# Tile-by-tile ends, quartered projection weights, spread POOL splits in a one-layer hybrid encoder step

## The chip, the core and the metric

The kernel runs on one core of a Trainium2 chip. A core has a matrix engine (TensorE, PE in the profile, with its weight loads as PEld) and three elementwise engines: VectorE (DVE), ScalarE (ACT) and GpSimd (POOL). The sync engine (SP) issues the DMA transfers. Each engine works through its own queue in order, and semaphores tie the queues together. The metric is the device time of one execution in microseconds (us). Smaller is better.

## The reference

One layer on 1024 prompt frames and 64 frames of a running stream, model width 1024, all in float32:

```python
hp = macaron_half(xp, ln1_g, ln1_b, ffn1_w_gate, ffn1_w_up, ffn1_w_down)
qa, ka, va, qi, ki, wi, qb, kb, vb, lfb = project(hp, pos, w_in, b_f)
mp = mixer(qa, ka, va, qi, ki, wi, qb, kb, vb, lfb)
hp = layer_norm(ALPHA * hp + mp @ w_out, ln2_g, ln2_b)
xp = macaron_half(hp, ln3_g, ln3_b, ffn2_w_gate, ffn2_w_up, ffn2_w_down)
...
def macaron_half(x, g, b, w_gate, w_up, w_down):
    return layer_norm(ALPHA * x + 0.5 * swiglu(x, w_gate, w_up, w_down), g, b)
```

The feed-forward width is 2816. The mixer has eight heads A (sparse: an indexer scores all keys with a weighted sum of Relus and the best 256 are attended, with a partial rotary embedding on the first 16 of 64 dimensions) and eight heads B (forgetting attention with a cumulative log gate). The new keys, values and gates are outputs too.

## The kernel before

**Tiles.** The 1088 rows are nine tiles t = 0..8 of 128 rows; tile 8 holds the 64 streaming rows. Each float32 factor of a product is split into a high part (a cast on ACT into the matmul type) and a low part (value minus high, on DVE or POOL; `split`, line 107), and a product is three matmuls: high x high, low x high, high x low. In the names an h or l at the end marks the parts: wh and wl, mh and ml.

**Feed-forward.** Each of the two feed-forward blocks is `ffn_a` (gate and up, line 203) and `ffn_b` (down, line 591). Both use a Strassen-like scheme over blocks of tiles 0 to 3 and 4 to 7: operand sums such as T1, T2, T3, T4 are made once, in `Strassen.put` (line 167), by subtracting a tile's normed row block zz and its partner's, fetched again from DRAM as zt. `body0` (line 258) is the first piece of `ffn_a`; its matmuls are called fa0 (fa in the profile), fs for the sample tile, fy for what follows, and its intermediate copies p are taken from PSUM by ACT into the buffers "ssum" (four of them). `ffn_b` runs seven products P1, P2, P3, P6, P5, P7, P4, each over six pairs of blocks of the inner dimension and four tiles; the matmuls are called fbP, with weights mh, ml and hidden values lh, ll. The first pairs of a product go over all four tiles in turn, its last `late` ones tile by tile, so that a tile's result is added (`evict`, line 674) while the next tile runs. With the last product, P4, the rows get their final norm (`finish`, `ln_tail`: lines 529 to 541 on DVE) and go out as y_prompt.

**Projection.** `in_proj` (line 1047) goes through eleven groups of columns of w_in, at most 328 wide, each over the tiles. `load_w` (973) fetches and splits the weights of the next group when tile `ahead` has been issued: as two blocks (wst) or three (ist), whose cast and subtraction stand in the queues at that place. Beside groups 2 and 3 run the indexer's scores, `idx_step`: matmuls iq, the Relu `rt` on ACT (line 1144), and sums on DVE and POOL. `rope_apply` (945) rotates a tile's heads with six small operations. `tsplit` (1061) transposes results through PSUM (ts...), from where ACT takes them (hl, ft).

**Attention and w_out.** Attention works through units of heads and query blocks, jobs B first and then jobs A. POOL scales each unit's exponentials e by 1/sum (line 1681). Outputs of jobs B are parked in DRAM and fetched again while jobs A run (`fetch_out`, name kept); POOL splits them into xh and xl (lines 1697 and 1698). After that `gemm_b` (432) multiplies with w_out in three groups of three tiles, adds the residual and norms (`zz_post`), and `emit_s` (1991 ff.) writes each tile to h2d and puts it into the operands of the second feed-forward.

**Order.** The order on each engine is drawn up when the program is built, by the framework's scheduler from the program order and its own cost estimates. The code sets priorities by where a step is written: generators put on `todo` are advanced by `pump` between matmuls, and `tc.issue_after(x)` holds an instruction behind x. A tile of a buffer pool waits until the buffer's last user is done.

Of the kernel before, what the change touches and what calls it, by code (L numbers as in the profile page):

```python
# [47 lines left out]
def hybrid_step(ctx: ExitStack, tc: tile.TileContext, i, o):  # L48
# [57 lines left out]

    def split(hi, lo, src):
        S.copy(hi, src)  # L108
        V.tensor_tensor(lo, src, f(hi), ALU.subtract)  # L109

# [34 lines left out]
    class Strassen:  # L145
# [20 lines left out]

        def put(self, t, z, hf, zt=None):
            if t == 8:
                put_xs(turned(t, z, hf), hf)
            elif t < 4:  # L170
                self.set("B21" if hf else "B11", t, turned(t, z, hf))
            elif hf == 0:
                self.more()
                self.set("B22", t, turned(t, z, 1))
                G.tensor_tensor(zt[:, 0:512], z[:, 0:512], zt[:, 0:512], ALU.subtract)
                self.set("T1", t, turned(t, zt, 0))
            else:
                G.tensor_tensor(z[:, 0:512], z[:, 512:1024], z[:, 0:512], ALU.subtract)
                G.tensor_tensor(z[:, 512:1024], z[:, 512:1024], zt[:, 0:512], ALU.subtract)
                G.tensor_tensor(zt[:, 512:1024], zt[:, 512:1024], z[:, 512:1024], ALU.subtract)  # L180
# [21 lines left out]

    def ffn_a(xo, wg, wu, hd, wd, during, pre=()):
        xo.sums()
# [53 lines left out]
        def body0(pss):  # L258
            Rs, Xs, old = [], [], []
            for u in range(2):  # L260
                raw = raws.pop((0, u)) if (0, u) in raws else raw_of(wg, wu, 0, u)
                R = []
                for q in range(2):
                    if u == 0:
                        h_, l_ = (wp.tile([P, 1024], F32R, tag=tg, name=tg) for tg in ("wh", "wl"))
                    else:
                        h_, l_ = (v.rearrange("p s c -> p (s c)")[:, q * 1024:(q + 1) * 1024] for v in (xo.sh, xo.sl))
                    split(h_, l_, raw[q].rearrange("p k c -> p (k c)"))
                    R.append([q4(h_), q4(l_)])
# [162 lines left out]
    def gemm_b(nk, get, w, pre, post, rate=1, tail=2, room=None, last=False):  # L432
        for g in range(3):
            skew = tail if g == 2 else 2
            order = (2, 0, 1) if g == 2 else (0, 1, 2)
            acc = []
# [508 lines left out]
    def rope_apply(t, ot, c0, nh):  # L945
        r = rows_of(t)
        v = ot[:r, c0:c0 + nh * HD].rearrange("p (h d) -> p h d", h=nh)
        x1, x2 = v[:, :, 0:8], v[:, :, 8:16]
        cosb = rope[:r, t, 0:1, :].to_broadcast([r, nh, 8])
        sinb = rope[:r, t, 1:2, :].to_broadcast([r, nh, 8])  # L950
        a, b = (att.tile([P, 4, 8], F32, tag=n, name=n, bufs=2) for n in ("ra", "rb"))
# [5 lines left out]
        E.tensor_tensor(x1, x1, b[:r, :nh], ALU.subtract)  # L957
        E.tensor_tensor(x2, x2, a[:r, :nh], ALU.add)

# [13 lines left out]
    def load_w(c0, n, store, eng):
        def sp2(hi, lo, src):
            S.copy(hi, src)
            eng.tensor_tensor(lo, src, f(hi), ALU.subtract)

        if store == "w":
            us = []
            for u in range(2):  # L980
                st = wp.tile([P, 1024], F32, tag="st", name="wst")
                DMA.dma_start(st.rearrange("p (a b) -> p a b", a=4),
                              w_in[u * 512:(u + 1) * 512, c0:c0 + n].rearrange("(k p) c -> p k c", p=P))
                wh = wp.tile([P, 1024], F32R, tag="wh", name="wh")
                wl = wp.tile([P, 1024], F32R, tag="wl", name="wl")
                sp2(wh, wl, st)
                us.append((wh, wl))
# [662 lines left out]
    def attn_soft(ht, qp, ops):  # L1650
# [28 lines left out]
        for q in range(2):  # L1679
            n = P * (2 * qp + q + 1)  # L1680
            G.tensor_scalar(es[q][:, :n], es[q][:, :n], su2[:, q:q + 1], 1.0, ALU.mult, ALU.mult)  # L1681
        return es
# [395 lines left out]
```

## Time and profile before

| | us |
|---|---|
| median of 3 runs | 2279.86 (2279.32 to 2284.34) |
| profiled execution | 2278.69 |
| its span | 2276.9 |
| PE busy | 2186.9 |
| DVE busy | 1489.8 |
| ACT busy | 963.0 |
| POOL busy | 906.4 |

The first feed-forward takes the span's first 750 us, the projection with the indexer and the top-k search runs to about 1064, attention to 1429, the product with w_out to 1530, and the second feed-forward to the end. In the lists below a row of a timeline gives start and length in us, engine, line, operation and tiles (output <- inputs), and in brackets the idle time of the engine before it and what ended that. A clock below 1.00 in a table by stretch says that PE was granted less than its full clock for part of it.

### The profile page before, as it was taken

The numbers are of one execution on the slowest core, as the hardware profiler recorded it, in microseconds if no ns is written. First come the engines' busy times: TensorE is split into PE (matmuls) and PEld (weight loads), VectorE is DVE, ScalarE is ACT, GpSimd is POOL, SyncE is SP. The second block draws the span as 40 slices with busy tenths as digits, with TensorE's granted clock in tenths as the row PEclk, the third lists the DMA queues.
The fourth block names the chain that finished last, engine by engine and source line by source line (L and its number), as shares of the span: only waits on it lengthen the run. The fifth ranks groups of instructions, "written<-read, shape, count | busy, mean of one in ns | idle before, by whom it ended". The sixth has DMA issues, their size and how long they took to land.

```text
span 2276.9 us, 33875 instructions
## 1 busy us (share of the span) xinstructions
PE 2186.9 (96%) x11832; PEld 1878.7 (83%) x11832; DVE 1489.8 (65%) x2359; ACT 963.0 (42%) x1776; POOL 906.4 (40%) x1058
## 2 busy tenths in 40 slices
PE   8999999999999999999898999998999999999997
PEld 7888888887888989998897787886888888877886
DVE  4576675556569656686857887675555655654678
ACT  4333333334344356733666787333333333333332
POOL 4556556541011323352546655023564564530011
PEclk9999999999999999999999999998999999999999
DMA  6566544458556343554667533553443443477554
GB/s 200 180 210 217 186 153 148 140 178 304 166 196 208 108 121 118 161 151 133 171 172 202 146 93 113 166 183 113 149 160 117 158 156 117 159 258 237 179 182 152
DMA packets 330297, 379.31 MB, mean 167 GB/s; under 512 B 43440, under 2 KB 226160, under 8 KB 330124
## 3 DMA queue, kind: packets, MB, share of 16 engines
q1 hardware_dynamic: 330122, 377.13, 52.8%
q8 instruction: 94, 1.54, 0.3%
q14 instruction: 81, 0.65, 0.1%
HBM read 256.51 MB, written 120.53 MB: 166 GB/s over the span
## 4 chain that ended last, share of the span: by engine, by line
PE 45%; DVE 5%; issue 1%; ACT 1%; DMA 1%; POOL 1%; SPq 0%; DVEq 0%; ACTq 0%; POOLq 0%
PE fa L114 11%; PE fbP L114 8%; PE fz L114 5%; PE fy L114 3%; PE gb L114 3%; PE pq L114 2%; PE acc L114 2%; PE ip L114 2%; PE pt L1744 2%; PE fs L114 2%; DVE pp L109 1%; PE fbs L114 1%; PE gb_a L114 1%; PE gb_b L114 1%; PE sacc L114 1%
## 5 line engine op out<-in xcount | busy, mean ns | idle before, releaser
L114 PE MATMUL fbP<-ml,lh 128*128 128x512 f32 x616 | 238.6, 391 | 1.5 <-DVE ml L109 1.5
L114 PE MATMUL fbP<-mh,ll 128*128 128x512 f32 x616 | 237.9, 390 | 2.1 <-DVE ll L109 2.1
L108 ACT CAST wh<-wst 128x1024 fp32r<-128x1024 f32 x108 | 113.3, 1052 | 286.6 <-PE fs L114 108.6
L114 PE MATMUL fbP<-mh,lh 128*128 128x512 f32 x616 | 224.2, 392 | 2.6 <-ACT lh L108 1.7
L109 DVE TENSOR_TENSOR wl<-wst,wh 128x1024 fp32r<-128x1024 f32 x108 | 159.5, 1478 | 69.8 <-ACT wh L108 60.6
L331 DVE TENSOR_TENSOR Sl<-S,Sh 128x512 fp32r<-128x512 f32 x160 | 161.8, 1018 | 29.3 <-ACT Sh L330 27.7
L108 ACT CAST lh<-raw 128x1024 fp32r<-128x1024 f32 x84 | 82.4, 981 | 228.4 <-PE fbP L114 195.1
L662 POOL TENSOR_TENSOR zz<-u,zz 128x512 f32<-128x512 f32 x16 | 25.6, 1613 | 379.6 <-DVE u L684 268.8
L330 ACT CAST Sh<-S 128x512 fp32r<-128x512 f32 x160 | 97.4, 618 | 187.4 <-PE fa L114 113.9
L109 DVE TENSOR_TENSOR ll<-raw,lh 128x1024 fp32r<-128x1024 f32 x84 | 100.0, 1191 | 115.2 <-ACT lh L108 115.0
L327 POOL TENSOR_TENSOR S<-wst 128x512 f32<-128x512 f32 x80 | 125.1, 1564 | 113.5 <-DVE Sl L331 52.0
L327 POOL TENSOR_TENSOR S<-wst,S 128x512 f32<-128x512 f32 x40 | 61.6, 1539 | 239.0 <-issue 235.4
L114 PEld LDWEIGHTS fbP<-mh,lh 128*128 128x128 f32 x616 | 115.7, 189 | 27.7 <-ACT lh L108 2.0
L114 PEld LDWEIGHTS fbP<-ml,lh 128*128 128x128 f32 x616 | 115.5, 188 | 27.7 <-DVE ml L109 4.1
L114 PEld LDWEIGHTS fbP<-mh,ll 128*128 128x128 f32 x616 | 115.6, 188 | 26.8 <-DVE ll L109 2.9
L1681 POOL TENSOR_SCALAR e<-e,su 128x128 f32<-128x128 f32 (+7 forms) x128 | 99.4, 789 | 77.3 <-DVE su L1678 61.6
L114 PE MATMUL acc<-pp,vs 128*128 128x256 f32 (+1 forms) x640 | 114.8, 300 | 9.0 <-DVE pp L109 5.6
L109 DVE TENSOR_TENSOR pp<-pt,pp 128x512 fp32r<-128x512 f32 (+1 forms) x160 | 99.1, 631 | 29.4 <-ACT pp L108 28.0
L114 PE MATMUL ip<-iwh,xh 128*128 128x256 f32 (+3 forms) x384 | 114.7, 299 | 2.0 <-ACT o L1043 0.9
L114 PE MATMUL ip<-iwl,xh 128*128 128x256 f32 (+3 forms) x384 | 111.4, 290 | 0.0
L114 PE MATMUL ip<-iwh,xl 128*128 128x256 f32 (+3 forms) x384 | 111.3, 290 | 0.0
L114 PEld LDWEIGHTS acc<-pp,vs 128*128 128x128 f32 x640 | 91.1, 196 | 14.5 <-DVE pp L109 7.9
(507 smaller groups left out, 6746.9 us busy)
## 6 DMA issues: line engine op xcount, KB each, us to landing
wst<-ffn_w_gate SPq DMA_DIRECT2D x88, 256.0 KB
wst<-ffn_w_up SPq DMA_DIRECT2D x88, 256.0 KB
w<-ffn_w_down SPq DMA_DIRECT2D x44, 512.0 KB
raw<-ffn_w_down SPq DMA_DIRECT2D x40, 512.0 KB
wst<-w_out SPq DMA_DIRECT2D x24, 512.0 KB
hd0T<-w SPq DMA_DIRECT2D x44, 256.0 KB
hd0S<-ringz SPq DMA_DIRECT2D x44, 256.0 KB
hd1T<-w SPq DMA_DIRECT2D x44, 256.0 KB
```

The source lines that it names most:

```text
L108: S.copy(hi, src)
L109: V.tensor_tensor(lo, src, f(hi), ALU.subtract)
L114: last_mm[:] = [PE.matmul(out, lhsT, rhs, start=start, stop=stop, skip_group_check=more).ins]
L327: G.tensor_tensor(t, ss[0] if x is None else x, ss[1] if y is None else y, op)
L330: S.copy(hi, t)
L331: V.tensor_tensor(lo, t, f(hi), ALU.subtract)
L662: eng.tensor_tensor(z_of(t, d), acc, z_of(t, d), ALU.add)
L1681: G.tensor_scalar(es[q][:, :n], es[q][:, :n], su2[:, q:q + 1], 1.0, ALU.mult, ALU.mult)
L1744: PE.transpose(pt[:, m * P:(m + 1) * P], e[:, kt * P:(kt + 1) * P], ident)
```

## The change

Six edits, in the order of the program:

1. **Quartered weights.** `load_w` fetches most groups of w_in as four quarters of 128x512 into the "ssum" buffers (group 3 also has an eighth column block, wex) and puts their splits on a list, wsp. `in_proj` takes one piece per tile from the second tile after `ahead` on, and what is left at the next group's start. Before, they were whole blocks in the ring "st", split on the spot. Group 2 is asked for one tile sooner (5 for 6).
2. **Rope** in four operations: both halves are multiplied at once.
3. **tsplit** takes its PSUM from two pools in turn where it took one.
4. **Fetched B outputs**: each put of `kept` is held behind the scaling of the unit before it.
5. **Second feed-forward's start**: the last group of `gemm_b` goes over tiles 6, 7, 8 in order, and their norms and puts are advanced tile after tile, five turns each, where tile 8 came first and the three took turns. zt is two halves in "ssum" (before one tile in the ring "wl"). The subtractions of tiles 7 and 8 are on DVE, those of 4 to 6 stay on POOL. The low halves of `body0`'s weights go from DVE to POOL.
6. **Last ffn_b**: P4 finishes one tile after another over all six pairs; four of its pairs are loaded in P5 and P7 into other buffers (slot8).

```diff
-    def split(hi, lo, src):
+    def split(hi, lo, src, E=V):
         S.copy(hi, src)
-        V.tensor_tensor(lo, src, f(hi), ALU.subtract)
+        E.tensor_tensor(lo, src, f(hi), ALU.subtract)
...
-                    split(h_, l_, raw[q].rearrange("p k c -> p (k c)"))
+                    split(h_, l_, raw[q].rearrange("p k c -> p (k c)"), first_eng)
...
-            order = (2, 0, 1) if g == 2 else (0, 1, 2)
+            order = (0, 1, 2)
...
-            for j in (0, 0, 0, 1, 1, 1, 0, 0, 2, 2, 2, 1, 1, 2, 2):
+            turns = (0, 0, 0, 0, 0, 1, 1, 1, 1, 1, 2, 2, 2, 2, 2) if g == 2 else \
+                (0, 0, 0, 1, 1, 1, 0, 0, 2, 2, 2, 1, 1, 2, 2)
+            for j in turns:
...
+            NP = len(PAIRS)
+            FAR = 4 if last else 0
+            far = [steps.index(("P4", q)) for q in range(FAR)]
...
+                pool = None if i in far else hb_
...
-                late = 3 if p == "P4" else 2
+                late = (NP if last else 3) if p == "P4" else 2
...
                     load(i + q + 2)
+                    if last and p in ("P5", "P7") and q % 3 == 1:
+                        load(far[2 * (p == "P7") + q // 3])
...
-                        product(acc[t], t, i + q, False, q == len(PAIRS) - 1)
+                        with ExitStack() as es:
+                            if last and p == "P4" and t and q == 0:
+                                es.enter_context(tc.issue_after(last_mm[0]))
+                            product(acc[t], t, i + q, q == 0, q == len(PAIRS) - 1)
...
-        E.tensor_tensor(a[:r, :nh], x1, sinb, ALU.mult)
-        E.tensor_tensor(b[:r, :nh], x2, sinb, ALU.mult)
-        E.tensor_tensor(x1, x1, cosb, ALU.mult)
-        E.tensor_tensor(x2, x2, cosb, ALU.mult)
-        E.tensor_tensor(x1, x1, b[:r, :nh], ALU.subtract)
-        E.tensor_tensor(x2, x2, a[:r, :nh], ALU.add)
+        E.tensor_tensor(a, x12, cosb, ALU.mult)
+        E.tensor_tensor(b, x12, sinb, ALU.mult)
+        E.tensor_tensor(x12[:, :, 0], a[:, :, 0], b[:, :, 1], ALU.subtract)
+        E.tensor_tensor(x12[:, :, 1], a[:, :, 1], b[:, :, 0], ALU.add)
...
+            for k in range(0, KD, 2):
+                st = mp.tile([P, 512], F32, tag="ssum", name="wst", bufs=4).rearrange("p (k c) -> p k c", k=2)
+                DMA.dma_start(st, w_in[k * P:(k + 2) * P, c0:c0 + 256].rearrange("(k p) c -> p k c", p=P))
+                rest.append((slice(k, k + 2), slice(0, 256), st))
...
+            wsp.extend(lambda p=p: one(*p) for p in rest)
...
         in_weights(gi)
+        while wsp:
+            wsp.pop(0)()
         for t in tiles:
             h = proj_tile(gi, t, mid)
+            if wsp and t > ahead + 1:
+                wsp.pop(0)()
...
-        pt = (big if hp_[0] is pc else sm)("ts" + name)
+        nts[0] += 1
+        pt = (big if hp_[0] is pc and nts[0] % 2 else sm)("ts" + name)
...
-    in_proj(1, (4, 5, 6, 7), 6)
+    in_proj(1, (4, 5, 6, 7), 5)
...
         if jn > A_JOB:
-            next(kept, None)
+            with tc.issue_after(last_pool[0]):
+                next(kept, None)
...
-            zt = wp.tile([P, 1024], F32, tag="wl", name="zt")
-            DMA.dma_start(zt, h2d[t - 4])
-        xo2[0].put(t, z, 0, zt)
+            zt = [mp.tile([P, 512], F32, tag="ssum", name="zt", bufs=4) for _ in range(2)]
+            for c in range(2):
+                DMA.dma_start(zt[c], h2d[t - 4][:, c * 512:(c + 1) * 512])
+        E = V if t >= 7 else G
+        xo2[0].put(t, z, 0, zt, E)
```

**What moves on the engines.** First PE at the end of body0's fa matmuls; xt are transposes into PSUM, `ident,zz` of the normed tile and `ident,zt` of the fetched one. Before, all of tile 8's and tile 7's transposes follow the last fa matmul, and fs follows them:

```order
7125 L114 MATMUL fa_1_17138<-B21h,Sl 128x512
7126 L129 MATMUL xt_0_17079<-ident,zz 128x64 x4
7127 L129 MATMUL xt_1_17086<-ident,zz 128x64 x4
7128 L129 MATMUL xt_1_17123<-ident,zz 128x128 x4
7129 L129 MATMUL xt_0_17131<-ident,zt 128x128 x4
7130 L129 MATMUL xt_1_17157<-ident,zz 128x128 x4
7137 L129 MATMUL xt_1_17213<-ident,zt 128x128 x4
7138 L114 MATMUL fs_16982<-wh,xsa 128x256
```

Now tile 6's last (7092) and tile 7's first four groups stand ahead of the last 36 fa matmuls, twelve of B11 and 24 of B21, with tile 7's last and tile 8's between these two:

```order
7092 L129 MATMUL xt_0_17052<-ident,zt 128x128 x4
7093 L129 MATMUL xt_1_17091<-ident,zz 128x128 x4
7094 L129 MATMUL xt_0_17099<-ident,zt 128x128 x4
7095 L129 MATMUL xt_1_17121<-ident,zz 128x128 x4
7096 L129 MATMUL xt_0_17128<-ident,zz 128x128 x4
7097 L114 MATMUL fa_1_17156<-B11h,Sh 128x512
7108 L114 MATMUL fa_1_17156<-B11h,Sl 128x512
7109 L129 MATMUL xt_0_17135<-ident,zt 128x128 x4
7110 L129 MATMUL xt_0_17174<-ident,zz 128x64 x4
7111 L129 MATMUL xt_1_17181<-ident,zz 128x64 x4
7112 L114 MATMUL fa_1_17156<-B21h,Sh 128x512
```

At the same place POOL now has the four low halves (wl, Sl) among the subtractions of tiles 4, 5 and 6 (lines 175 to 180); in before there were none on POOL:

```order
736 L175 TENSOR_TENSOR zt<-zz,zt 128x512 x2
737 L178 TENSOR_TENSOR zz<-zz 128x512 x2
738 L109 TENSOR_TENSOR wl<-wst,wh 128x1024
739 L179 TENSOR_TENSOR zz<-zz,zt 128x512
740 L180 TENSOR_TENSOR zt<-zt,zz 128x512
741 L109 TENSOR_TENSOR wl<-wst,wh 128x1024
742 L109 TENSOR_TENSOR Sl<-wst,Sh 128x1024 x2
743 L179 TENSOR_TENSOR zz<-zz,zt 128x512
744 L180 TENSOR_TENSOR zt<-zt,zz 128x512
745 L175 TENSOR_TENSOR zt<-zz,zt 128x512
```

Second, ACT beside the indexer, in before: the casts of group 3's weights (iwh<-ist) stand between Relus (rt) of width 640.

```order
475 L1144 ACTIVATE rt<-iq_1_7380 128x640
478 L1078 ACTIVATE ft<-tskb 128x256
479 L975 CAST iwh<-ist 128x3x264 x2
480 L1144 ACTIVATE rt<-iq_2_7445 128x640
481 L975 CAST iwh<-ist 128x2x264
482 L1144 ACTIVATE rt<-iq_3_7462 128x640
```

Now its pieces (from wex and wst) stand ahead of the first Relus, those of width 384:

```order
443 L1075 COPY ot<-ip_7_7041 128x328
444 L991 CAST iwh<-wex 128x8x8
445 L991 CAST iwh<-wst 128x2x256 x2
447 L991 CAST iwh<-wst 128x2x256
449 L991 CAST iwh<-wst 128x2x256
450 L1186 ACTIVATE rt<-iq_0_7115 128x384
```

Third, POOL in the attention, in before: the splits of the fetched outputs stand in one run, ahead of the scaling of e (line 1681) of width 640.

```order
633 L1697 TENSOR_SCALAR xh_4342<-kept 128x256
634 L1698 TENSOR_TENSOR xl_4337<-kept,xh_4336 128x256
635 L1697 TENSOR_SCALAR xh_4336<-kept 128x256
636 L1697 TENSOR_SCALAR xh_4338<-kept 128x256
637 L1681 TENSOR_SCALAR e<-e,su 128x640
638 L1681 TENSOR_SCALAR e<-e,su 128x768
639 L1698 TENSOR_TENSOR xl_4339<-kept,xh_4338 128x256
640 L1698 TENSOR_TENSOR xl_4341<-kept,xh_4340 128x256
```

Now one or two pairs follow each unit's two scalings (line 1725 in the changed program):

```order
601 L1725 TENSOR_SCALAR e<-e,su 128x384
602 L1725 TENSOR_SCALAR e<-e,su 128x512
603 L1741 TENSOR_SCALAR xh_4336<-kept 128x256
604 L1742 TENSOR_TENSOR xl_4337<-kept,xh_4336 128x256
606 L1725 TENSOR_SCALAR e<-e,su 128x640
607 L1725 TENSOR_SCALAR e<-e,su 128x768
608 L1741 TENSOR_SCALAR xh_4338<-kept 128x256
610 L1742 TENSOR_TENSOR xl_4339<-kept,xh_4338 128x256
```

More of the change, by code (lines that the diff above doesn't have):

```diff
@@ L201, in hybrid_step, with ffn_a @@
     TT = SEQ + DEC
-    def ffn_a(xo, wg, wu, hd, wd, during, pre=()):
+    def ffn_a(xo, wg, wu, hd, wd, during, pre=(), first_eng=V):
         xo.sums()
@@ L623, in pair @@
                 st = fetch(src, n, tags[0])
-                hl = [pool.tile([P, 1024], F32R, tag=tg, name=tg, bufs=3) for tg in tags[1:]]
+                if pool is None:
+                    both = slot8("tl" + tags[1]).rearrange("p (s c) -> p s c", s=2)
+                    hl = [both[:, 0], both[:, 1]]
+                else:
+                    hl = [pool.tile([P, 1024], F32R, tag=tg, name=tg, bufs=3) for tg in tags[1:]]
                 split(hl[0][:, :n * 512], hl[1][:, :n * 512], st[:, :n * 512])
                 return [x.rearrange("p (k c) -> p k c", k=2) for x in hl]
+            NP = len(PAIRS)
+            FAR = 4 if last else 0
+            far = [steps.index(("P4", q)) for q in range(FAR)]
             def load(i):
-                if i >= len(steps):
+                if i >= len(steps) or i in ops:
                     return
@@ L632, in load @@
                 A, B = OPS[p]
-                ops[i] = pair(w_src(B, q), q, ("st", "mh", "ml"), hb_)
-                ops[i] += pair(hd[A][q][0:PAIRS[q][1]].rearrange("k p c -> p k c"), q, ("wl", "lh", "ll"), hb_)
+                pool = None if i in far else hb_
+                ops[i] = pair(w_src(B, q), q, ("st", "mh", "ml"), pool)
+                ops[i] += pair(hd[A][q][0:PAIRS[q][1]].rearrange("k p c -> p k c"), q, ("wl", "lh", "ll"), pool)
             def load_s(r):
@@ L768, in put @@
         def put(t, hf):
-            xo.put(t, at[t], hf, at.get(t - 4))
+            xo.put(t, at[t], hf, [at[t - 4][:, c * 512:(c + 1) * 512] for c in range(2)])
             yield
@@ L947, in rope_apply @@
         v = ot[:r, c0:c0 + nh * HD].rearrange("p (h d) -> p h d", h=nh)
[L948 to L951, printed above, removed]
+        x12 = v[:, :, 0:16].rearrange("p h (s d) -> p h s d", s=2)
+        cosb, sinb = (rope[:r, t, q:q + 1, :].rearrange("p (a b) d -> p a b d", a=1).to_broadcast([r, nh, 2, 8])
+                      for q in range(2))
+        a, b = (att.tile([P, 4, 2, 8], F32, tag=n, name=n, bufs=2)[:r, :nh] for n in ("ra", "rb"))
         E = rp_[0]
-        E.tensor_tensor(a[:r, :nh], x1, sinb, ALU.mult)
-        E.tensor_tensor(b[:r, :nh], x2, sinb, ALU.mult)
-        E.tensor_tensor(x1, x1, cosb, ALU.mult)
-        E.tensor_tensor(x2, x2, cosb, ALU.mult)
-        E.tensor_tensor(x1, x1, b[:r, :nh], ALU.subtract)
-        E.tensor_tensor(x2, x2, a[:r, :nh], ALU.add)
+        E.tensor_tensor(a, x12, cosb, ALU.mult)
+        E.tensor_tensor(b, x12, sinb, ALU.mult)
+        E.tensor_tensor(x12[:, :, 0], a[:, :, 0], b[:, :, 1], ALU.subtract)
+        E.tensor_tensor(x12[:, :, 1], a[:, :, 1], b[:, :, 0], ALU.add)
     pend_h = []
@@ L971, in flush @@
             pend_h.pop(0)()
+    wsp = []
     def load_w(c0, n, store, eng):
@@ L976, in sp2, with later, one @@
             eng.tensor_tensor(lo, src, f(hi), ALU.subtract)
+        def later(dst):
+            rest = []
+            if n > 256:
+                ex = mp.tile([P, 512], F32, tag="hsh", name="wex")[:, 0:KD * (n - 256)].rearrange(
+                    "p (k c) -> p k c", k=KD)
+                DMA.dma_start(ex, w_in[:, c0 + 256:c0 + n].rearrange("(k p) c -> p k c", p=P))
+                rest.append((slice(0, KD), slice(256, n), ex))
+            for k in range(0, KD, 2):
+                st = mp.tile([P, 512], F32, tag="ssum", name="wst", bufs=4).rearrange("p (k c) -> p k c", k=2)
+                DMA.dma_start(st, w_in[k * P:(k + 2) * P, c0:c0 + 256].rearrange("(k p) c -> p k c", p=P))
+                rest.append((slice(k, k + 2), slice(0, 256), st))
+            def one(ks, cs, st):
+                hi, lo = dst(ks, cs)
+                sp2(hi, lo, st)
+            wsp.extend(lambda p=p: one(*p) for p in rest)
         if store == "w":
@@ L980, in load_w @@
             for u in range(2):
-                st = wp.tile([P, 1024], F32, tag="st", name="wst")
-                DMA.dma_start(st.rearrange("p (a b) -> p a b", a=4),
-                              w_in[u * 512:(u + 1) * 512, c0:c0 + n].rearrange("(k p) c -> p k c", p=P))
                 wh = wp.tile([P, 1024], F32R, tag="wh", name="wh")
                 wl = wp.tile([P, 1024], F32R, tag="wl", name="wl")
-                sp2(wh, wl, st)
                 us.append((wh, wl))
+            later(lambda ks, cs: [x.rearrange("p (k c) -> p k c", k=4)[:, ks.start % 4:ks.start % 4 + 2, cs]
+                                  for x in us[ks.start // 4]])
             def wt(k):
@@ L995, in load_w @@
             iwh = pw_[1].tile([P, KD, pw_[2]], F32R, tag="iwh", name="iwh")
-            for k0, kn in ((0, 2), (2, 2), (4, 2), (6, 2)) if hp_[0] is None else ((0, 3), (3, 3), (6, 2)):
+            if hp_[0] is not None and n < 328:
+                later(lambda ks, cs: (iwh[:, ks, cs], iwl[:, ks, cs]))
+            for k0, kn in ((0, 2), (2, 2), (4, 2), (6, 2)) if hp_[0] is None else \
+                    ((0, 3), (3, 3), (6, 2)) if n == 328 else ():
                 if hp_[0] is None:
@@ L1613, in hybrid_step @@
     hp_[0] = None
+    while wsp:
+        wsp.pop(0)()
     pend_9 = [proj_tile(9, t) for t in range(2)]
@@ L1635, in vst @@
         return v.rearrange("p a b -> p (a b)")
-    last_act, last_dve = [], []
+    last_act, last_dve, last_pool = [], [], []
     def normalise(su, *parts):
```

21 lines of the change are left out of this document (11 added, 10 removed).

## The prediction

> **What bounds the kernel now.** I read the page's span and busy times first.
>
> ```profile
> span 2276.9 us, 33875 instructions
> PE 2186.9 (96%) x11832; PEld 1878.7 (83%) x11832; DVE 1489.8 (65%) x2359; ACT 963.0 (42%) x1776; POOL 906.4 (40%) x1058
> ```
>
> TensorE (PE) is busy for 96% of the span, and the change leaves its matmuls and transposes as many as before. So a gain can come from three places only: time in which PE waits, work that PE does at a reduced clock, and the time behind its last matmul. The second view is the busy table by stretch. The columns are length, busy time of PE, PE's weight loads, DVE, ACT and POOL, then the granted PE clock.
>
> ```profile
> 755.00:772.00 17.00, 15.40 (x103) 14.25 (x103) 14.86 (x31) 7.12 (x15) 6.47 (x20) 0.76 0.43 145
> 836.00:846.00 10.00, 6.17 (x27) 6.17 (x28) 5.95 (x7) 5.30 (x9) 0.00 (x0) 0.66 0.38 112
> 1018.00:1045.00 27.00, 21.62 (x153) 20.84 (x152) 20.01 (x50) 11.66 (x29) 7.50 (x7) 0.87 0.60 173
> 1240.00:1250.00 10.00, 7.36 (x31) 6.11 (x32) 2.97 (x11) 3.67 (x12) 9.81 (x17) 0.66 0.82 181
> 1562.00:1576.00 14.00, 6.85 (x31) 6.45 (x32) 4.81 (x7) 4.60 (x7) 7.83 (x7) 0.52 0.33 109
> 1580.00:1630.00 50.00, 50.00 (x230) 41.41 (x229) 24.41 (x26) 14.77 (x23) 28.20 (x19) 1.00 0.35 112
> 2200.00:2256.00 56.00, 55.45 (x243) 45.25 (x243) 48.95 (x74) 20.92 (x26) 6.00 (x4) 1.00 0.52 175
> ...
> 2264.00:2277.00 13.00, 0.00 (x0) 0.00 (x0) 9.32 (x23) 0.41 (x2) 0.00 (x0) 0.57 0.41 161
> ```
>
> The row of 1580 is how most of the kernel looks: PE full, clock 1.00. The other rows are the places that the edits touch. There PE both waits and runs slowly. As an estimate, busy time times (1 - clock) is what the reduced clock costs: 15.40 x 0.24 = 3.7 us in the first, 6.17 x 0.34 = 2.1, 21.62 x 0.13 = 2.8, 7.36 x 0.34 = 2.5 and 6.85 x 0.48 = 3.3 in the fifth. The third view names PE's waits: total, count, longest.
>
> ```profile
> PE xt L129 <- POOL zt L175: 5.6, 1, 5.6
> ...
> PE iq L114 <- ACT rt L1144: 4.7, 2, 4.5
> ...
> PE xt L129 <- POOL zz L179: 3.7, 2, 2.7
> ...
> PE tsqb L1064 <- ACT ft L1078: 3.2, 2, 2.3
> PE pt L1744 <- POOL e L1681: 2.5, 1, 2.5
> ...
> PE ip L114 <- ACT o L1043: 0.9, 1, 0.9
> ...
> PE tsqi L1064 <- POOL ot L957: 0.6, 1, 0.6
> ```
>
> **The change part by part.** All terms stand against the profiled execution, 2278.7 us (the span and 1.8 us around it); the median of the runs, 2279.9, lies 1.2 above it.
>
> *Tile-by-tile ends.* Rows of PE and DVE at the end of before:
>
> ```profile
> 2263.10 0.39 PE L114 MATMUL fbP<-mh,ll 128*128 128x512 f32 x1
> ...
> 2256.73 1.29 DVE L662 TENSOR_TENSOR zz<-fbP,zz 128x512 f32<-128x512 f32 x2 [5.08 <-PE fbP L114]
> ...
> 2263.53 0.69 DVE L662 TENSOR_TENSOR zz<-fbP,zz 128x512 f32<-128x512 f32 x1
> ...
> 2264.34 0.69 DVE L529 BATCH_NORM_STATS2 bst<-zz 128x6 f32<-128x512 f32 x1
> ...
> 2268.84 1.27 DVE L539 SCALAR_TENSOR_TENSOR zz<-zz,bmv,gb 128x1024 f32<-128x1024 f32 x1
> 2270.04 0.21 DVE L535 SCALAR_TENSOR_TENSOR bve<-brs,bve 128x1 f32<-128x1 f32 x1
> ...
> 2272.07 1.28 DVE L541 SCALAR_TENSOR_TENSOR zz<-zz,brs,gb 128x1024 f32<-128x1024 f32 x1
> ```
>
> The last product is added at 2263.53 and DVE ends at 2273.35: 9.8 us, since the first two tiles of P4 are added only from 2256.73 and four norms pile up behind. Now each tile gets its 33 matmuls in one go; at the 0.22 us of the row of 1580 (230 in 50 us) they take 7.2 us, longer than a norm. So behind the last matmul stands one tile's own chain: 0.69 (L662) + 0.69 (L529) + 1.27 (L539) + 1.28 (L541) + six small ones of about 0.2 = 5.1 us. **4.7 us** go. What is left behind DVE, the last y_prompt transfer (2273.35 to 2276.9), stays. P5 and P7 load four of P4's pairs early, two each; in P7 they take the place of two that it loaded for P4 before. In the row of 2200 PE idles 0.55 us and DVE has 7 us left of 56, so I cost this at nothing; with DVE late, 1 to 2 us come back.
>
> *FFN2's start.* Rows of POOL and DVE before, then of the chain of waits (start, length, engine, output):
>
> ```profile
> 1524.26 2.29 POOL L180 TENSOR_TENSOR zt<-zt,zz 128x512 f32<-128x512 f32 x1
> ...
> 1565.16 1.26 POOL L175 TENSOR_TENSOR zt<-zz,zt 128x512 f32<-128x512 f32 x1 [1.49 <-DMA zt<-h2d]
> ...
> 1533.68 1.22 DVE L109 TENSOR_TENSOR wl<-wst,wh 128x1024 fp32r<-128x1024 f32 x1
> ...
> 1549.20 3.66 DVE L541 SCALAR_TENSOR_TENSOR zz<-zz,brs,gb 64x1024 f32<-64x1024 f32 x3
> ```
>
> ```profile
> 1531.78 2.56 PE fa L114 x10
> 1534.34 0.44 PE xt L129 x4
> ...
> 1541.16 8.20 PE fa L114 x36
> ...
> 1560.53 4.50 DMA zt<-h2d
> ...
> 1573.09 5.30 PE fs L114 x32
> ```
>
> The norms of tiles 6, 7 and 8 end together at 1552.9, all 96 fa matmuls are done by then, and tile 7's transposes wait for a 4.5 us transfer and POOL. The wait rows above give 5.6 + 3.7 us, the reduced clock 3.3 more. In the new order tiles 6, 7, 8 finish one after another, and 36 fa matmuls stand behind most of tile 7's transposes. Without any wait PE needs from 1531.8 on 96 x 0.228 = 21.9 us (36 in 8.20) and 20 transpose groups of 0.44 = 8.8: fs could begin at 1562.5, not at 1573.1, so 10 to 11 are to be had.
>
> What the edit puts in the way: four subtractions of 128x1024 go from DVE (1.22) to POOL, where no row shows that shape. Two of 128x512 bound it: 2 x 1.26 = 2.5 below, 2 x 2.29 = 4.6 above. I take 2.5: with DVE lighter, POOL is nearer to the 1.26 of its later row. They stand ahead of tile 5's last two and tile 6's four subtractions, 10 us on POOL that PE hides only while fa work lasts; and tile 7's fetched halves wait for the buffers that tile 6's leave. POOL, free for this at about 1524, has 4 x 2.5 + 7 x 1.27 = 18.9 us before tile 6's L179 is through, 1543 at the earliest; with tile 6's own fetch about 1546. Half a transfer (2.3) to a whole (4.5) brings tile 7's operand at 1548 to 1550.5, a DVE subtraction 1551. PE gets there after 60 fa and 13 groups, at about 1551. So I keep 2 us of waiting: **9 us** go. With 4.6 for each, 8.4 us come back.
>
> *Quartered weights.* The rows of ACT and PE:
>
> ```profile
> 836.11 0.85 ACT L975 CAST iwh<-ist 128x792 fp32r<-128x792 f32 x1 [2.40 <-DMA ist<-w_in]
> 838.32 0.85 ACT L975 CAST iwh<-ist 128x792 fp32r<-128x792 f32 x1 [1.35 <-DMA ist<-w_in]
> 839.08 0.70 ACT L1144 ACTIVATE rt<-iq 128x640 f32<-128x640 f32 x1
> ...
> 839.83 1.43 PE L114 MATMUL iq<-kid,qsi 128*128 128x384 f32 x4 [4.54 <-ACT rt L1144]
> ```
>
> ACT stands at a cast for a transfer, the Relu (rt) behind it is late, and PE waits 4.5 us and then runs slowly for 2.1. In the new order these casts come piece by piece ahead of the first narrow rt. **6 us** of the 6.6 go. Around 1018 to 1045 PE waits for ft (3.2 in all) and loses 2.8 to the clock; fewer blocked casts on ACT and the second PSUM buffer of tsplit help with it: I take **2** of 6, between 0 and 6.
>
> *Rope* drops two of six POOL steps per tile. Two waits of 0.9 and 0.6 are near it and 3.7 of reduced clock: **1.5**, between 0 and 5.
>
> *Fetched B outputs.*
>
> ```profile
> 1239.07 0.73 POOL L1698 TENSOR_TENSOR xl<-kept,xh 128x256 fp32r<-128x256 f32 x1
> 1239.77 0.40 POOL L1697 TENSOR_SCALAR xh<-kept 128x256 fp32r<-128x256 f32 x1
> ...
> 1242.65 1.68 POOL L1681 TENSOR_SCALAR e<-e,su 128x640 f32<-128x640 f32 x2
> ```
>
> Twelve pairs of 0.40 + 0.73 = 13.6 us ran in a burst ahead of the scaling of e; POOL was busy 9.81 of 10 us and PE waited 2.5 and lost 2.5 to the clock. Spread, one pair stands behind each unit's scaling, where the next scaling comes 1.1 us later at worst. **4 of 5** go.
>
> Sum: 4.7 + 9 + 6 + 2 + 1.5 + 4 = 27. From 750 to 1530 every engine's order is drawn up anew. Waits below 1 us such as the two above will come up at other places; I take off 4. So 23 go: 2278.7 - 23 = 2255.7, and with the median's 1.2 **2257**.
>
> [...] In the row of 755 the clock is 0.76, while PE's longest waits there are the 0.9 and the 0.6. [...]
>
> **The rivals.**
> *POOL late at FFN2's start.* The four low halves at 4.6 us, or the chain of buffers from tile 6 to 7, give the 9 us back: 2266. For it: the 2.29 row, with DVE busy beside it. Against: DVE is lighter there by 4.9 us. 0.18.
> *Every short wait is free of clock loss.* The spells at 755 and 1018 go too (3.7 + 2.8, of which 2 are counted) and the 4 us of new waits don't come: 2257 - 8.5 = 2248. Against it stands the row of 755. 0.12.
> *The change only moves waits.* The tail's 4.7 come, the others are given back in the projection and attention, whose PE waits have many releasers: 2275 to 2279. For it: POOL and ACT get the same work. 0.09.
> *Slower: pieces late at the group boundaries.* A group's weights are split piece by piece behind its predecessor's tiles; if the last piece lands late, PE waits at the boundary for a transfer (4.5), a cast (0.85) and a POOL subtraction (1.26): 6.6 us, at seven boundaries. It decides from four of them on (26 against 23); at five 33 are lost and the time is 2290. For it: ACT waited 2.40 and 1.35 for such transfers in the rows above. Against: pieces are asked for at the third of nine tiles. 0.07.
>
> **How the numbers follow.** The forecast 2257 has 0.54. Of the cases the first three are faster by over 0.2% (4.6 us, about what a measurement of this kernel tells from no change): 0.54 + 0.18 + 0.12 = 0.84; moved waits 0.09 are the same, the last 0.07 slower. The range 2245 to 2273 takes in the forecast, its POOL rival, the second rival and the bounds of tsplit and rope; it leaves out the last two, 0.16.
>
> **What would show it.** Right: behind the last fbP matmul some 5 us of DVE, not 9.8; fs beginning about 10 us sooner after the first fa; no rt wait of 4.5 near 840 and a clock near 1.00 there; no kept rows in a burst. Wrong: a long wait of xt for zt or of fa for p (the copies share the buffers of zt) behind POOL's low halves; PE waiting for iwl or wl at a group's first ip; new rows under 0.9 in the clock column.

## The result, and the profile after

| | before | after |
|---|---|---|
| median, us | 2280.62 (4 runs) | 2254.47 (2251.3 to 2258.03, 4 runs) |
| ratio | | 0.989, 95% interval 0.987 to 0.9909 |
| span of the profiled execution | 2276.9 | 2249.5 |

The changed kernel is 26 us faster, where 23 were forecast. One run of u_w below, 3133 us at a granted clock of 0.64, was a slow one and is left out of its median. The changed kernel's busy times, from the page:

```profile
span 2249.5 us, 33828 instructions
PE 2181.2 (97%) x11832; PEld 1873.4 (83%) x11832; DVE 1489.8 (66%) x2353; ACT 964.6 (43%) x1791; POOL 907.7 (40%) x979
```

PE has as many instructions as before, and the other engines as much work. So the gain is waiting, and where it went is read best by cutting both traces at the same instructions: PE's first row of ip, tkf, pq, gb, fs (second feed-forward) and fbP (second `ffn_b`), and its last fbP. Lengths in us, worked out from these rows' starts:

| stretch | before | after | difference |
|---|---|---|---|
| start to ip (first feed-forward) | 750.4 | 749.8 | -0.6 |
| ip to tkf (projection, indexer) | 286.8 | 275.3 | -11.5 |
| tkf to pq | 33.2 | 33.2 | 0.0 |
| pq to gb (attention) | 354.4 | 349.1 | -5.3 |
| gb to fs (w_out, body0's fa) | 147.9 | 145.3 | -2.6 |
| fs to fbP | 453.4 | 451.7 | -1.7 |
| fbP to the last fbP | 237.0 | 235.7 | -1.3 |
| behind the last fbP | 13.8 | 9.4 | -4.4 |

The edits touch nothing in the first row. Over the fourteen traces of this study it lies between 749.8 and 754.0, so a profiled execution carries some 4 us of chance before the change begins to matter. The row before last lies between 235.5 and 238.9 in them and is of that kind too. The busy table by stretch, of the changed kernel, at the places of the prediction (columns as there; line numbers of the changed program are up to 47 higher):

```profile
755.00:772.00 17.00, 15.37 (x106) 14.52 (x106) 14.85 (x33) 6.88 (x16) 7.74 (x18) 0.84 0.30 112
818.00:828.00 10.00, 8.23 (x46) 7.24 (x46) 7.57 (x15) 6.44 (x15) 2.67 (x3) 0.83 0.88 258
1006.00:1033.00 27.00, 27.00 (x227) 26.80 (x226) 19.84 (x50) 13.34 (x36) 6.97 (x9) 1.00 0.53 151
1230.00:1245.00 15.00, 14.10 (x105) 12.99 (x104) 13.44 (x33) 12.25 (x30) 9.03 (x15) 1.00 0.60 155
1509.00:1531.00 22.00, 19.29 (x103) 15.53 (x101) 21.88 (x41) 9.91 (x19) 17.36 (x8) 1.00 0.47 147
1531.00:1545.00 14.00, 10.65 (x39) 8.90 (x40) 9.52 (x14) 4.72 (x9) 7.59 (x6) 0.51 0.57 179
```

The third row is the answer to 1018 of before: PE is busy for all of it, at full clock. The fourth answers to the burst at 1240: POOL is no longer full. The last two are the second feed-forward's start, and there the clock is as low as it was (0.51, before 0.52). PE's waits say the same:

```profile
...
PE pq L114 <- ACT e L1716: 6.8, 9, 3.3
...
PE xt L129 <- DVE zz L179: 2.4, 1, 2.4
PE fbP L114 <- DVE ll L109: 2.1, 2, 1.0
PE iq L114 <- ACT rt L1186: 2.0, 2, 1.8
...
PE xt L129 <- DVE T2l L109: 1.8, 1, 1.8
```

The wait of iq for rt is down from 4.7 to 2.0, those for ft, tk_bad and the scaling of e are gone, and xt waits for DVE where it waited for POOL. One wait has grown: pq's for ACT's e, in the attention, was 3.3 us in all and 0.7 at most before. At the end, DVE has one tile's norm behind the last product:

```profile
2240.59 0.69 DVE L673 TENSOR_TENSOR zz<-fbP,zz 128x512 f32<-128x512 f32 x1 [2.40 <-PE fbP L114]
2241.32 0.69 DVE L531 BATCH_NORM_STATS2 bst<-zz 128x6 f32<-128x512 f32 x1
...
2242.36 1.27 DVE L541 SCALAR_TENSOR_TENSOR zz<-zz,bmv,gb 128x1024 f32<-128x1024 f32 x1
...
2244.38 1.28 DVE L543 SCALAR_TENSOR_TENSOR zz<-zz,brs,gb 128x1024 f32<-128x1024 f32 x1
```

From 2240.59 to 2245.66 are 5.1 us, as the prediction added up; the idle 2.40 ahead of the first row shows that the tile before was through.

### The profile page after: what moved, and what is told of

Its sections match the earlier page's. It is cut to its first block, busy times and chain, and to the rows that moved or that the text cites. A ratio compares the mean times of both kernels' runs of the same rounds, so it can differ in the third digit from the quotient of the medians.

```text
span 2249.5 us, 33828 instructions
## 1 busy us (share of the span) xinstructions
PE 2181.2 (97%) x11832; PEld 1873.4 (83%) x11832; DVE 1489.8 (66%) x2353; ACT 964.6 (43%) x1791; POOL 907.7 (40%) x979
## 5 line engine op out<-in xcount | busy, mean ns | idle before, releaser
L114 PE MATMUL fbP<-ml,lh 128*128 128x512 f32 x584 | 226.3, 391 | 1.9 <-DVE ml L109 1.7
L114 PE MATMUL fbP<-mh,ll 128*128 128x512 f32 x584 | 225.7, 390 | 2.1 <-DVE ll L109 2.1
L114 PE MATMUL fbP<-mh,lh 128*128 128x512 f32 x584 | 212.6, 392 | 2.7 <-ACT lh L108 1.7
L114 PEld LDWEIGHTS fbP<-ml,lh 128*128 128x128 f32 x584 | 109.6, 188 | 27.1 <-DVE ml L109 4.8
L114 PEld LDWEIGHTS fbP<-mh,lh 128*128 128x128 f32 x584 | 109.1, 188 | 26.7 <-ACT mh L108 2.4
L114 PEld LDWEIGHTS fbP<-mh,ll 128*128 128x128 f32 x584 | 109.6, 188 | 25.5 <-DVE ll L109 2.9
```

The source lines that it names most:

```text
L114: last_mm[:] = [PE.matmul(out, lhsT, rhs, start=start, stop=stop, skip_group_check=more).ins]
```

## The experiments

Each run of the first kind undoes one edit of the change. Beside the time stand the stretches that the edits can touch, since the rest moves by chance; each is read from one profiled execution.

| kernel | median, us | ratio to before, 95% | ip to tkf | pq to gb | gb to fs | end |
|---|---|---|---|---|---|---|
| the change | 2254.5 | 0.9890 (0.9870 to 0.9909) | 275.3 | 349.1 | 145.3 | 9.4 |
| u_tail | 2259.7 | 0.9915 (0.9900 to 0.9931) | 273.9 | 354.3 | 145.1 | 14.1 |
| u_ffn2 | 2258.3 | 0.9910 (0.9893 to 0.9928) | 275.0 | 350.3 | 147.3 | 9.1 |
| u_w | 2260.8 | 0.9918 (0.9903 to 0.9934) | 285.3 | 352.8 | 146.6 | 9.3 |
| u_ts | 2252.6 | 0.9888 (0.9872 to 0.9905) | 278.5 | 349.7 | 144.2 | 9.4 |
| u_kept | 2262.9 | 0.9925 (0.9909 to 0.9941) | 274.1 | 356.8 | 142.8 | 9.6 |
| u_rope | 2251.7 | 0.9874 (0.9855 to 0.9893) | 274.5 | 351.7 | 145.4 | 9.4 |
| u_first | 2260.0 | 0.9904 (0.9884 to 0.9923) | 276.0 | 352.7 | 145.3 | 9.4 |
| zt_hsh | 2252.4 | 0.9872 (0.9848 to 0.9896) | 277.3 | 350.4 | 141.3 | 9.4 |
| zt_hsh_v | 2253.4 | 0.9891 (0.9876 to 0.9906) | 277.2 | 349.2 | 141.1 | 9.4 |
| zt_hsh_G | 2255.3 | 0.9893 (0.9877 to 0.9909) | 277.2 | 350.1 | 143.4 | 9.4 |
| zt_hsh_no8 | 2251.0 | 0.9887 (0.9870 to 0.9903) | 274.3 | 349.4 | 137.9 | 9.4 |
| b_w | 2274.3 | 0.9979 (0.9970 to 0.9988) | 274.8 | 356.7 | 149.3 | 14.2 |

The kernel before, measured again beside these runs, had medians from 2278.3 to 2280.6, and of the undone versions none has an interval clear of that of the change (u_kept's touches it). So what a part is worth is read from its stretch, and the medians only support it.

**The tail undone (u_tail).**

```diff
-            FAR = 4 if last else 0
+            FAR = 0
-                late = (NP if last else 3) if p == "P4" else 2
+                late = 3 if p == "P4" else 2
```

> The change with its sixth edit undone: P4 again goes over its tiles in turn for three pairs and loads nothing early. My theory (the tail shrinks by one tile's own norm chain): 4.7 us slower than the change, so about 2259, with some 9.8 us from the last product's addition to DVE's end again. Rival (the gain at the end of the profile is another's, and the extra early loads cost PE as much as they save): within 2 us of the change, 2253 to 2257.

The median is 5.3 us up and the end 4.7 us longer. The term stands, and the four early pairs cost nothing that shows. DVE's rows of this kernel, the last addition and the end of the last norm, 9.8 us apart as expected:

```profile
2246.97 0.69 DVE L673 TENSOR_TENSOR zz<-fbP,zz 128x512 f32<-128x512 f32 x1
...
2255.51 1.28 DVE L543 SCALAR_TENSOR_TENSOR zz<-zz,brs,gb 128x1024 f32<-128x1024 f32 x1
```

**The second feed-forward's start undone (u_ffn2).**

```diff
-            order = (0, 1, 2)
+            order = (2, 0, 1) if g == 2 else (0, 1, 2)
-        E = V if t >= 7 else G
+        E = G
-    ffn_a(xo2[0], ..., first_eng=G)
+    ffn_a(xo2[0], ...)
```

(and zt in one tile of "wl", turns mixed.)

> The change with its fifth edit undone as a whole: tile 8 first and turns mixed, zt in one tile of the ring wl, all subtractions of the tiles on POOL, low halves of body0 on DVE. My prediction gave this edit 9 us: the time would be about 2263. The rival that the profile of the change suggests: fa to fs takes 43.2 us there against 42.1 in the kernel before, so only the 3.7 us ahead of the first fa are the edit's: about 2258.

The rival had it: 2258.3. gb to fs is 2.0 us longer and fs to fbP, 453.1, is 1.4 longer. Of 9 us the edit brings about 4. From the first fa to fs it brings nothing: 41.6 us here, 43.2 in the change. These two lengths don't hold the same work, since 20 transposes that stand ahead of the first fa here stand behind it in the change; that is also most of the 3.7 us ahead of it.

**The quarters undone (u_w), and alone on the kernel before (b_w).** `load_w` is that of the other kernel, with its part of `in_proj`.

> The change with its first edit undone: weights of the projection groups again in whole blocks split on the spot. My prediction gave it 6 us, at the indexer: 2260, with PE's wait for rt of 4 to 5 us near 840 back. The rival from the profile of the change, where 7.9 us more vanish between the last iq and the first search matmul (groups 4 to 8): the quarters are worth 10 to 12 us, 2265, and the stretch from the last iq to the first tkf is back at 126 us from 118.

The stretch from ip to tkf is 10.0 us longer, as the rival said; the median is 6.4 up, as my own 6 said. Cut at PE's last iq, the part behind it is back at 126.9 us from 118.1, and only 1.3 of the 10 lie ahead of it, at the indexer, where the traces with the quarters scatter from 155.7 to 159.1. PE's waits between 820 and 1060 in u_w, and two of ACT's rows there:

```profile
PE tsqa L1087 <- DVE ot L972: 4.6, 1, 4.6
PE iq L114 <- ACT rt L1167: 4.5, 1, 4.5
PE tsqb L1087 <- ACT ot L1056: 1.5, 1, 1.5
```

```profile
1019.85 1.05 ACT L108 CAST fx_ch<-fx_sc 8x1024 fp32r<-8x1024 f32 x1 [5.96 <-DVE fx_sc L1512]
...
1031.40 0.83 ACT L991 CAST iwh<-ist 128x768 fp32r<-128x768 f32 x1 [2.52 <-DMA ist<-w_in]
```

Not one place but two: beside the wait at the indexer, ACT stands 6 us for a row of the log gate (fx_sc) from DVE and then 2.5 for weights, and PE waits for what is queued behind them. In the change the same cast stood for 1.42:

```profile
1009.91 1.05 ACT L108 CAST fx_ch<-fx_sc 8x1024 fp32r<-8x1024 f32 x1 [1.42 <-DVE fx_sc L1531]
```

> The kernel before with the quartered weights alone. The run without them lost 10 us between the first ip and the first tkf. If the quarters do this by themselves, that stretch, 286.9 us in the kernel before, becomes 276 to 279 and the time 2269 to 2273 (with the kernel before at 2280). My prediction's term of 6 would give 2274. Rival (they work only together with the second PSUM pool and the shorter rope): 2276 or more.

Alone, the quarters take the stretch to 274.8: all 12 us, without the second PSUM pool and the shorter rope, so the rival fell. The median falls by only 4 (2274.3 against 2278.3 beside it), which is what my term of 6 gave and less than the stretch promised. Of the missing 8 the traces place 1.8 between tkf and pq, 2.3 in the attention and 1.4 between gb and fs. The attention, from pq to gb, of the kernel before and of b_w:

```profile
1070.50:1424.90 354.40, 325.26 (x2276) 292.06 (x2275) 268.79 (x607) 246.47 (x606) 201.09 (x368) 0.97 0.56 153
```

```profile
1063.30:1420.00 356.70, 331.97 (x2272) 297.83 (x2271) 267.44 (x606) 245.77 (x605) 201.05 (x368) 0.94 0.57 152
```

The same work keeps PE busy 6.7 us longer at a clock of 0.94. Whether attention costs more in this order or by chance was not settled.

**tsplit's PSUM (u_ts) and rope (u_rope) undone.**

```diff
-        pt = (big if hp_[0] is pc and nts[0] % 2 else sm)("ts" + name)
+        pt = (big if hp_[0] is pc else sm)("ts" + name)
```

> The change with its third edit undone: tsplit takes its PSUM from one pool again. My prediction gave it, with the quarters, 2 us around 1018 to 1045: at most 2256.5. Rival: the second pool is what frees the 7.9 us between the last iq and the first tkf, then 2262 with that stretch back at 126 us.

> The change with its second edit undone: six rope operations for four. My prediction gave it 1.5 us: about 2256. Rival (POOL is not waited for there): 2254.5, with the stretch from the first ip to the last iq as long as in the change, 157.2 us.

Neither is slower than the change. u_ts has its stretch at 278.5, 3.2 longer, but zt_hsh, which keeps the edit, has 277.3. From the last iq to tkf u_ts takes 119.5 us, where the change and the other undone versions with the quarters take 118.1; but b_w, which lacks the second pool too, takes 118.2. Both edits are worth nothing that these runs resolve.

**The fetched outputs undone (u_kept).**

```diff
-            with tc.issue_after(last_pool[0]):
-                next(kept, None)
+            next(kept, None)
```

> The change with its fourth edit undone: the splits of the fetched B outputs are free to run in a burst again. My prediction gave it 4 us: about 2258.5, with PE's wait for the scaling of e near 1240 back. Rival (other waits of the attention take over, whatever POOL does): within 1 us of the change's 2254.5.

The median is 8.4 us up. The wait for the scaling of e is back, and so is the burst; PE's wait and the table by stretch of u_kept:

```profile
PE pt L1788 <- POOL e L1725: 2.4, 1, 2.4
```

```profile
1236.00:1244.00 8.00, 5.89 (x26) 5.17 (x26) 1.53 (x6) 2.18 (x6) 7.81 (x13) 0.57 0.82 191
```

Attention takes 349.1 to 354.3 us in the eleven traces that have this edit (mean 350.9) and 354.4 to 356.8 in the three that don't (mean 356.0): 5 us. Two of these three, the kernel before and b_w, lack other edits too. The other 3 of the median have no place in the traces.

**Why the second feed-forward's start gave half.** First the low halves alone (u_first):

```diff
-    ffn_a(xo2[0], ..., first_eng=G)
+    ffn_a(xo2[0], ...)
```

> The change with only the low halves of body0 put back on DVE. Theory A (POOL is what makes tiles 6 and 7 late: its low halves took 2.4 to 3.2 us, and DVE's L541 took 3.44 us beside them): fa to fs, 43.2 us in the change, becomes 39 to 41 and the time 2251 to 2253. Rival B (with them DVE has 4.9 us more ahead of the norms and the first fa starts later): the 3.7 us ahead of the first fa are lost and the time is 2256 to 2259.

By its time, 2260.0, B would hold, but gb to fs is 145.3 us, as in the change (102.9 to the first fa and 42.4 behind it, for 102.0 and 43.2); the difference lies in stretches that this edit can't touch (start 752.9, attention 352.7). Neither theory: the move is worth nothing. POOL's and DVE's rows of the change, and then of u_first, point to the reason:

```profile
1513.58 4.75 POOL L109 TENSOR_TENSOR Sl<-wst,Sh 128x1024 fp32r<-128x1024 f32 x2 [0.92 <-ACT Sh L108]
...
1515.97 3.44 DVE L541 SCALAR_TENSOR_TENSOR zz<-zz,bmv,gb 128x1024 f32<-128x1024 f32 x1
```

```profile
1523.30 1.20 DVE L109 TENSOR_TENSOR Sl<-wst,Sh 128x1024 fp32r<-128x1024 f32 x1
...
1529.48 1.27 DVE L541 SCALAR_TENSOR_TENSOR zz<-zz,bmv,gb 128x1024 f32<-128x1024 f32 x1
```

DVE is spared 1.2 us a piece and takes 3.44 for 1.27 on a norm beside POOL's Sl. That this balances the whole gain was not tested by itself.

Then zt's buffers, with the second half in a pair of its own (zt_hsh); on top of that the low halves on DVE (zt_hsh_v), tile 7's subtractions on POOL (zt_hsh_G), and no norm of tile 8 behind w_out (zt_hsh_no8):

```diff
-            zt = [mp.tile([P, 512], F32, tag="ssum", name="zt", bufs=4) for _ in range(2)]
+            zt = [mp.tile([P, 512], F32, tag="ssum", name="zt", bufs=4),
+                  mp.tile([P, 512], F32, tag="hsh", name="zt")]
```

> The change with zt's second half in a buffer pair of its own (hsh), so that tile 7 does not wait for tile 6's buffers nor the copies p for zt's. Theory C (the chain of buffers holds tile 7: its norm ended at 1529.0, its fetch was issued at 1531.5 and its first subtraction ran at 1534.7): fa to fs becomes 36 to 39 us and the time 2248 to 2251. Rival (DVE and the transposes' PSUM hold it all the same): fa to fs stays above 42 and the time at 2254.

> zt_hsh with body0's low halves back on DVE. Theory (what DVE saves by the move, 4.9 us, it loses again by running slower beside POOL): fa to fs stays within 1 us of zt_hsh's 39.3. Rival (with the chain of buffers gone DVE's own load decides): fa to fs 42 us or more and the time 3 us above zt_hsh's 2252.

> zt_hsh with tile 7's four subtractions on POOL, as those of tiles 4 to 6. If DVE is the bound, the 2.7 us taken from it shorten fa to fs to 37 to 38.5 us. Rival (tile 7's own chain is the bound, and POOL takes 1.27 us for each step instead of 0.68): fa to fs 40 to 42 us.

> zt_hsh without the norm of tile 8 behind w_out: the streaming rows enter the second feed-forward as the plain residual. This takes some 7 us of DVE out of the 22 in which it is full. Theory (DVE is the bound at this place): the wait of xt for T2l, 2.0 us, goes and fa to fs falls from 39.3 to 33 to 36 us, the time to about 2248. Rival (the transposes' own reduced clock and their PSUM bound it): fa to fs stays at 38 to 40.

Between the first rows of fa and fs lie 43.2 us in the change, 39.3 in zt_hsh (just above theory C's 36 to 39), 38.5 in zt_hsh_v, 41.7 in zt_hsh_G, where PE waits 2.2 and 2.3 for POOL's L179, and 35.8 in zt_hsh_no8. The times of 2248 to 2251 and 2248 that went with C and with the theory of zt_hsh_no8 were not reached (2252.4 and 2251.0).

Not all of these differences belong to the edits, for the clock differs too. Among the traces with the change's order at this place the length from fa to fs goes with how long the clock was half: 43.2 to 43.4 us with 13.7 us of it (the change, u_tail, u_w), 42.2 with 10.2 (u_ts, u_rope), 39.9 with none (u_kept). As an estimate from these, one us of half clock costs 0.24. zt_hsh and zt_hsh_G have 6.8 us of it and zt_hsh_no8 none, so without it the change would take 39.9, zt_hsh 37.7 and zt_hsh_no8 35.8: some 2 us for the chain of buffers, some 2 more for DVE's load, above all tile 8's norm, and by this estimate the rest is the clock. Tile 7 is better on DVE (39.3 us against zt_hsh_G's 41.7, with 6.8 us of half clock in both). In zt_hsh_no8 the clock stays up, but it did so in u_kept with that norm, so the norm isn't shown to be the reason. The table of zt_hsh_no8 by stretch, and zt_hsh's at the low clock:

```profile
1510.10:1531.00 20.90, 19.33 (x105) 15.32 (x103) 18.87 (x26) 10.11 (x19) 16.61 (x8) 1.00 0.63 196
1531.00:1546.00 15.00, 12.82 (x73) 10.60 (x74) 8.95 (x15) 5.44 (x12) 6.66 (x5) 1.00 0.30 114
```

```profile
1536.30:1543.10 6.80, 5.68 (x18) 4.82 (x19) 6.41 (x8) 1.89 (x4) 2.85 (x2) 0.50 0.29 60
```

zt_hsh and zt_hsh_v are the best full versions by this stretch, 4 us under the change with the clock counted in; their medians, 2252.4 and 2253.4, don't differ from its 2254.5 by more than the runs scatter.

## Why the prediction held, and where it did not

The range held the time and the forecast was 2.5 us above it. Its terms were off in both directions, and that the total came so near is in part luck: FFN2's start gave 5 us less than its term, while the 4 taken off for new waits, 2 more from the projection and 2 from stretches that no edit touches made up for it.

- **Tail, 4.7:** measured 4.4 in the trace and 5.3 by the run without it. Right, mechanism and size.
- **Quarters, 6 with 2 around 1018:** 10 to 12 in their stretch, 4 to 6 by the medians. The mechanism was right, the sizes were changed about. The indexer, which was to give 6, gave 3.6 in these traces (first ip to last iq, 160.8 before and 157.2 after; 2.0 of the wait for rt and a clock of 0.83 are left), and from the last iq to tkf 126.0 became 118.1: 7.9, where I took the place for another's and gave it 2 of 6 us. The stretch at 1018 lost all of its waits and low clock (21.62 busy of 27 at 0.87 became 27.00 of 27 at 1.00), and u_w and b_w show that the quarters do it: they clear ACT's and DVE's queues there too.
- **Fetched outputs, 4:** 5 in the attention.
- **Rope, 1.5, and the second PSUM pool:** nothing. The stretch at 755 hardly changed (15.37 busy at 0.84, before 15.40 at 0.76), so the rival that all such spells go was right at 1018 and wrong here.
- **FFN2's start, 9:** about 4, that is 2.6 up to fs and 1.7 behind it. The sign that I named, fs some 10 us sooner after the first fa, did not come: 43.2 us after it, before 42.1, with 20 more transposes between. The 1.7 had no term at all: before, the half clock lasted 3.6 us past fs, and in the change it ended ahead of it. The row by stretch of the kernel before, from fs on:

```profile
1572.70:1576.30 3.60, 3.60 (x18) 3.60 (x17) 3.35 (x6) 3.00 (x5) 0.00 (x0) 0.50 0.01 2
```

The step that failed is "with tile 6's own fetch about 1546", 14 us behind the first fa, from which the 2 us of waiting followed. It was a sum of POOL and the transfer, and DVE was not in it. PE's, DVE's and POOL's rows of the change:

```profile
1509.48 0.39 PE L114 MATMUL fa<-B11h,wh 128*128 128x512 f32 x1
...
1524.01 1.27 DVE L543 SCALAR_TENSOR_TENSOR zz<-zz,brs,gb 128x1024 f32<-128x1024 f32 x1
...
1530.18 1.27 POOL L179 TENSOR_TENSOR zz<-zz,zt 128x512 f32<-128x512 f32 x1
```

DVE, busy for 21.88 of 22 us, lets tile 6's norm go at 1525.3, and its L179 ends at 1531.45, 22 us behind the first fa. PE came to these transposes about when I had said, 18.3 us behind it, and found them late:

```profile
1527.54 0.40 PE L114 MATMUL fa<-B21h,wl 128*128 128x512 f32 x1
1529.78 0.63 PE L129 MATMUL xt<-ident,zt 128*128 128x128 f32 x4 [1.84 <-DVE T2l L109]
1531.51 1.97 PE L129 MATMUL xt<-ident,zz 128*128 128x128 f32 x8 [1.10 <-DVE B22l L109]
1533.88 1.11 PE L129 MATMUL xt<-ident,zt 128*128 128x128 f32 x4 [0.41 <-POOL zt L180]
...
1539.14 1.94 PE L129 MATMUL xt<-ident,zz 128*128 128x128 f32 x8 [2.44 <-DVE zz L179]
1540.73 0.78 PE L114 MATMUL fa<-B11h,Sh 128*128 128x512 f32 x1
```

The waits are 1.84 + 1.10 + 0.41 + 2.44 = 5.8 us, not 2; and the 3.3 of reduced clock that I let go came again, eight transposes taking 1.94 us where eight took 1.03 at 1523.94, at a clock of 1.00. The rival with POOL's low halves named the chain of buffers rightly, at some 2 us and what the clock adds, but its price for the low halves was not paid: my lower bound of 2.5 fits the rows of Sl (4.75 for two; one wl took 3.21). Two readings were wrong without harm: the kernel before has the shape on POOL, two rows of L976 with a mean of 2.67 us, and its last fa matmul ended at 1555.8, not by 1552.9.
- **New waits, 4 off:** some came, as pq's for ACT's e (3.5 us more), but others of the attention shrank (acc's for pp from 5.6 to 2.8), and no stretch of the change is longer than before. The slower rival did not come: PE's list has no long wait for a group's weights.
- **The clock at 1562, 0.52 in the prediction's table:** PE's wait of 5.6 us began at 1560.9, and the clock was 1.00 up to 1562.6 and 0.50 from 1562.7 on, 1.8 us into the wait. The kernel before by stretch:

```profile
1560.90:1562.60 1.70, 0.00 (x0) 0.00 (x0) 1.45 (x3) 0.67 (x2) 1.54 (x3) 1.00 0.60 104
1562.70:1566.40 3.70, 0.00 (x0) 0.00 (x0) 0.00 (x0) 0.00 (x0) 2.21 (x3) 0.50 0.83 300
```

## What to carry over

Put a load's conversion into a queue as small pieces, after the data has landed: in these kernels that made ip to tkf 10 to 12 us shorter (u_w, b_w). Casts that stood waiting for weights cost PE at two places 190 us apart: ACT stood 2.40 and 1.35 us at 836 and 838 of the kernel before, and PE 4.54 for the Relu queued behind them; in u_w it stood 2.52 at 1031. Before moving work from one elementwise engine to another, look how long each one's operations take beside the other's: here L541 took 3.44 us on DVE beside POOL's Sl, and 1.27 with Sl on DVE. And judge a part of a change by the stretch that it can touch: here the start alone scattered by 4 us, as much as most of the edits were worth. Look at the clock in that stretch too: with like orders of work, fa to fs took 43.2 to 43.4 us with 13.7 us of half clock and 39.9 with none.

## What was not expected of the hardware

**The same transposes, with and without the half clock.** From 1527.9 to 1540.7 of the change PE ran 32 transposes and no other matmul, with no wait above 2.44 us; the clock was half (0.50) from about 1531 to 1545. u_kept, whose edit lies in the attention, has the same 32 transposes from 1538.7 to 1550.0, with more waiting among them (7.1 us against 5.8, 2.56 at most), and its clock stays at 1.00. The two by stretch, the change first:

```profile
1527.90:1540.70 12.80, 7.01 (x33) 5.91 (x33) 11.23 (x18) 4.53 (x8) 6.38 (x4) 0.62 0.63 201
```

```profile
1538.70:1550.00 11.30, 4.24 (x33) 3.38 (x33) 10.95 (x18) 4.04 (x8) 5.71 (x4) 1.00 0.68 215
```

In zt_hsh the time without a matmul other than transposes is 1533.3 to 1539.0, with 12 of these, and the clock is half for 6.8 us. In zt_hsh_no8 no such time there is above 3.7 us, and the clock stays at 1.00. In the kernel before it was 17.0 us, and the clock was 0.50 for its last 10.0. So in the change the clock fell with no wait of PE above 2.44 us, but the length of such a time doesn't decide it alone, at 11.3 us with the clock at 1.00 in u_kept and 5.7 with half clock in zt_hsh; what does, these runs don't show.

**DVE and POOL side by side.** L541 took 3.44 us beside POOL's Sl in the change, and 1.27 in u_first, where Sl is on DVE. Which of the two takes longer differs. A row of DVE and one of POOL in the change:

```profile
1525.20 1.27 DVE L541 SCALAR_TENSOR_TENSOR zz<-zz,bmv,gb 64x1024 f32<-64x1024 f32 x1
```

```profile
1525.41 2.22 POOL L175 TENSOR_TENSOR zt<-zz,zt 128x512 f32<-128x512 f32 x1 [2.47 <-PE xt L129]
```

Here DVE keeps its 1.27 us, and POOL takes 2.22 for what it does in 1.27 at 1530.18. In both pairs the operation that began later is the long one, by a little less than what was left of the earlier: Sl's second piece lasted 2.36 us beyond the start of L541, and this L541 lasted 1.06 beyond the start of L175. u_kept shows both pairs again, at 3.45 and 2.22.
